# FFN up projections of the second block: seven products of sums of quarters in place of eight, in 14 of 16 chunks

## The chip, the cores and the metric

One core of one Trainium2 chip runs the kernel. The metric is device time in microseconds (us) of one execution; the median of the runs before the change is 3163.79 us (3163.3 to 3165.95, three runs).

## What is computed

Two transformer-like blocks of two layers each, on 512 tokens of 1024 features, in fp32. The second block, cut to what matters here:

```python
def squared_relu_mlp(x, w_up, w_down):
    return jnp.square(jax.nn.relu(x @ w_up)) @ w_down      # w_up 1024 x 4096, w_down 4096 x 1024

for i in range(2):
    y = dilated_attention_mixer(x, ...) if i == 0 else hgrn2_mixer(x, ...)
    x = layer_norm(DEEPNORM_ALPHA * x + y, ...)
    y = squared_relu_mlp(x, ffn_w_up[i], ffn_w_down[i])
    x = layer_norm(DEEPNORM_ALPHA * x + y, ...)
```

The first block has feed-forward layers of the same kind (`w_mlp1`, `w_mlp2`); the change leaves them alone.

## The kernel before

Every large product is made of three matmuls: each operand is split into a high and a low part (type fp32r), and `mm3` adds high x high, high x low and low x high into one PSUM bank (lines 165 to 167). The first operand of a matmul is the stationary one (its load is PEld in the profile), the second streams. A bank holds 128 x 512 fp32; the second block has eight banks (`pb2`).

Weights come in chunks of 1024 x 256 (or 512 x 512 for the down product): one DMA of 1 MB from SP's queue into `wr`, then `wchunk` makes the high part on ScalarE (line 193, `wh`) and the low part on VectorE (line 194, `wl`). `wr`, `wh` and `wl` have two buffers each. Small working tiles of 128 x 512 (`h`) have eight buffers, the large slots of 4 KB a partition (`t`) 27 in this block.

`ffn` (second block, called twice) calls `mlp` with width 512. There, hT are the normalised tokens, feature-major, as four pairs of tiles [128, 2, 512] for each of the two parts, made from four tiles of 128 tokens by `turn` (lines 434 and 436 scale, 253 and 254 split). `up` makes 128 features of the hidden layer: 8 x 3 matmuls into one bank, then relu and square on ScalarE (496, 497), and `split_to` on VectorE (249, 250). The first two chunks of 256 features run by halves of the tokens, so that the first half can start while the last tokens are still being normalised. Then come eight groups g: one up chunk, the down product of chunks 2g and 2g+1 (two halves c of the output, four token tiles each, 12 matmuls of 512 columns a bank, with two W2 loads), whose `sink` adds into the residual `xl` (1335, 1337), and one more up chunk. So the up chunk at the end of a group and the one at the start of the next stand back to back; there are 16 chunks, the last in the group before the last.

The order on each engine isn't written out by hand. The framework's scheduler lays the instructions out at build time, by readiness in its own model and by program order among what is ready, and each engine then works through its list in order. `later`, `tick` and `need` put off pieces of the program by counts.

Of the kernel before, what the change touches and what calls it, by code (L numbers as in the profile page):

```python
# [8 lines left out]
F32 = mybir.dt.float32  # L9
F32R = mybir.dt.float32r  # L10
I32 = mybir.dt.int32
AF = mybir.ActivationFunctionType
# [101 lines left out]
class Net:  # L114
# [367 lines left out]
        self.later(wait, go, key)  # L482


    def mlp(self, width, xT, w1, w2, ranges, tiles, sink, lag=3):
        nc = self.nc
        self.cut = 2

        def up(hc, w, f, c0, n):
            ps = self.bank()[:, :n]  # L490
            for k in range(8):
                self.mm3(ps, (w[0][:, k, f * 128:(f + 1) * 128], w[1][:, k, f * 128:(f + 1) * 128]),
                         self.kx(xT, k, c0, n), k == 0, k == 7)
            self.tick()
            r = self.half()[:, :n]
            nc.scalar.activation(r, ps, AF.Relu)  # L496
            nc.scalar.activation(r, r, AF.Square)  # L497
            self.split_to(hc[0][:, f, c0:c0 + n], hc[1][:, f, c0:c0 + n], r)

        hs = []  # L500

        def chunk():

            c0 = len(hs) * 256
            hs.append((self.slot([128, 2, width], F32R), self.slot([128, 2, width], F32R)))
            return hs[-1], self.wcols(w1, [(c0, c0 + 256)], alike=len(hs) > 2)

        def ups():
            if len(hs) < 16:
                h, w = chunk()  # L510
                for f in range(2):
                    for c0, n in ranges[1]:
                        up(h, w, f, c0, n)
                self.pump()

        first = [chunk(), chunk()]
        for c0, n in ranges[0]:
            self.need(*[("h", c) for c in range(c0, c0 + n, 128)])
            for h, w in first:
                for f in range(2):  # L520
                    up(h, w, f, c0, n)
        self.need()
        for g in range(8):
            ups()
            h = hs[2 * g:2 * g + 2]
            w = [None, None]
            for c, (tt, c0) in self.skew(tiles, lag if g == 7 else len(tiles)):
                if w[c] is None:
                    w[c] = self.wcols(w2[g * 512:(g + 1) * 512], [(c * 512, c * 512 + 512)], kt=4, alike=True)
                    self.pump()  # L530
                ps = self.bank()
                for k in range(4):
                    self.mm3(ps, (h[k // 2][0][:, k % 2, c0:c0 + 128], h[k // 2][1][:, k % 2, c0:c0 + 128]),
                             (w[c][0][:, k, :], w[c][1][:, k, :]), k == 0, k == 3)
                self.tick()
                sink(tt, c, g, ps)
            ups()
# [843 lines left out]
    def ffn(self, i, hT, last):  # L1381
        t = self.t
        rows = self.ln_rows("ffn", i)
        box = []

        def sink(j, c, g, ps):
            self.add_res(j, c * 512, 512, ps, g == 0)
            if g == 7:
                self.ln_stats(j, c)
                if c == 1:  # L1390
                    if not last and not box:
                        box.append(self.pairs(512))
                    self.ln_turn(j, "ffn", i, rows, None if last else box[0])

        self.mlp(512, hT, t["ffn_w_up_2"][i], t["ffn_w_down_2"][i], [[(0, 256), (256, 256)], [(0, 512)]],
                 [(j, j * 128) for j in range(4)], sink, 0 if last else 1)
        if last:
            self.need()
        return box[0] if box else None
# [531 lines left out]
```

## Time and profile before

| | us |
|---|---|
| median of three runs | 3163.79 |
| the profiled execution | 3167.63 |
| its span, first to last instruction | 3165.4 |
| TensorE / VectorE / ScalarE / GpSimd busy | 3102.1 / 1754.4 / 1344.6 / 376.5 |
| first FFN of the second block, chunk 2 to the end of group 6 | about 2215 to 2520 |
| second FFN, from chunk 2 on | about 2830 to 3130 |

A row of the trace gives a start, a duration, the engine, the line, what is written and read with the shapes, and in brackets how long the engine had been idle and what ended that. Matmul durations include the pipeline's depth and overlap; what a matmul costs in a stream is the distance between two starts.

### The profile page before, as it was taken

Reading aid. Unit: us, or ns where it says so; the run is one execution under the profiler, and the core shown is the slowest. Engines: PE = TensorE matmul, PEld = TensorE weight load, DVE = VectorE, ACT = ScalarE, POOL = GpSimd, SP = SyncE. Lnnn points to the kernel's source line nnn. Section 1 sums busy time; section 2 is a strip of 40 time slices with the busy share of each in tenths; the row PEclk is TensorE's granted clock in tenths of the full one; section 3 lists DMA queues with packets and bytes.
Section 4 is the critical chain, followed back from the end, with each engine's and each line's share of the span. In section 5 each row is a group of like instructions: output and inputs, shape, how many; then the busy total and the mean of one; then the engine's idle time right before and its main releaser. Section 6 shows DMA issues by size and latency. Waiting matters only on the chain.

```text
span 3165.4 us, 49101 instructions
## 1 busy us (share of the span) xinstructions
PE 3102.1 (98%) x20248; PEld 2633.0 (83%) x20248; DVE 1754.4 (55%) x3310; ACT 1344.6 (42%) x2533; POOL 376.5 (12%) x541
## 2 busy tenths in 40 slices
PE   7999999999999999999999999999999989989998
PEld 6977998888889879888888888888888878878887
DVE  5577454544456776555554544446444476664445
ACT  4566442222226665322245555555222266442222
POOL 4444000000004441000000000003000030030001
PEclk9999999999999999999999999999999999999999
DMA  7133223433322003233222222222333322222332
GB/s 224 44 104 107 68 84 118 131 109 108 119 73 67 12 14 94 93 97 103 93 97 94 80 68 67 81 70 67 106 96 104 98 67 67 89 81 98 93 94 79
DMA packets 246639, 281.67 MB, mean 89 GB/s; under 512 B 19534, under 2 KB 208400, under 8 KB 246416
## 3 DMA queue, kind: packets, MB, share of 16 engines
q1 hardware_dynamic: 244672, 273.54, 27.3%
q10 hardware_dynamic: 1584, 4.98, 0.4%
q8 instruction: 159, 2.61, 0.3%
q14 instruction: 64, 0.52, 0.1%
q0 software_dynamic: 160, 0.02, 0.0%
HBM read 276.42 MB, written 2.10 MB: 88 GB/s over the span
## 4 chain that ended last, share of the span: by engine, by line
PE 79%; issue 11%; DVE 5%; ACT 2%; POOL 1%; DMA 0%; SPq 0%; ACTq 0%; DVEq 0%; POOLq 0%
PE b L165 18%; PE b L167 17%; PE b L166 17%; PE s L165 5%; PE s L167 4%; PE s L166 4%; PE b L687 2%; PE b L671 2%; PE b L355 2%; PE s L649 1%; DVE t L254 1%; DVE wl L194 1%; PE b L1571 1%; PE b L1568 1%; PE b L1536 1%
## 5 line engine op out<-in xcount | busy, mean ns | idle before, releaser
L193 ACT ACTIVATE wh<-wr 128x2048 fp32r<-128x2048 f32 (+4 forms) x253 | 389.7, 1551 | 868.9 <-PE b L167 511.5
L194 DVE TENSOR_TENSOR wl<-wr,wh 128x2048 fp32r<-128x2048 f32 (+4 forms) x237 | 460.9, 1948 | 426.0 <-ACT wh L193 425.4
L165 PE MATMUL b<-wh,t 128*128 128x256 f32 (+2 forms) x2052 | 690.4, 337 | 0.8 <-ACT t L253 0.4
L166 PE MATMUL b<-wl,t 128*128 128x256 f32 (+2 forms) x2052 | 681.2, 332 | 4.1 <-DVE wl L194 4.1
L167 PE MATMUL b<-wh,t 128*128 128x256 f32 (+2 forms) x2052 | 681.3, 332 | 2.1 <-DVE t L254 2.1
L165 PE MATMUL b<-t,wh 128*128 128x512 f32 (+1 forms) x1696 | 625.9, 370 | 3.1 <-ACT t L253 3.0
L166 PE MATMUL b<-t,wh 128*128 128x512 f32 (+1 forms) x1696 | 616.8, 364 | 2.6 <-DVE t L254 2.6
L167 PE MATMUL b<-t,wl 128*128 128x512 f32 (+1 forms) x1696 | 617.5, 364 | 1.0 <-DVE wl L194 1.0
L165 PEld LDWEIGHTS b<-wh,t 128*128 128x128 f32 x2052 | 387.3, 189 | 45.6 <-issue 3.5
L166 PEld LDWEIGHTS b<-wl,t 128*128 128x128 f32 x2052 | 387.6, 189 | 42.3 <-DVE wl L194 4.9
L167 PEld LDWEIGHTS b<-wh,t 128*128 128x128 f32 x2052 | 387.1, 189 | 41.1 <-DVE t L254 3.0
L165 PEld LDWEIGHTS b<-t,wh 128*128 128x128 f32 x1696 | 321.7, 190 | 57.3 <-ACT t L253 4.0
L167 PEld LDWEIGHTS b<-t,wl 128*128 128x128 f32 x1696 | 322.2, 190 | 52.4 <-DVE wl L194 1.4
L166 PEld LDWEIGHTS b<-t,wh 128*128 128x128 f32 x1696 | 322.3, 190 | 50.4 <-DVE t L254 3.5
L249 DVE CAST t<-h 128x512 fp32r<-128x512 f32 (+1 forms) x176 | 66.2, 378 | 238.2 <-ACT h L497 238.0
L496 ACT ACTIVATE h<-b 128x512 f32<-128x512 f32 (+1 forms) x138 | 70.9, 513 | 219.1 <-PE b L167 219.1
L1202 DVE TENSOR_TENSOR h<-b,gate 128x512 f32<-128x512 f32 (+1 forms) x141 | 89.2, 632 | 113.7 <-PE b L167 113.7
L1337 DVE TENSOR_TENSOR xl<-xl,b 128x512 f32<-128x512 f32 x128 | 87.4, 684 | 112.3 <-PE b L167 112.3
L165 PE MATMUL s<-wh,t 128*128 128x256 f32 (+2 forms) x428 | 145.9, 341 | 2.0 <-ACT h L943 1.0
L166 PE MATMUL s<-wl,t 128*128 128x256 f32 (+2 forms) x428 | 143.0, 334 | 0.0
L167 PE MATMUL s<-wh,t 128*128 128x256 f32 (+2 forms) x428 | 142.9, 335 | 0.0
L1436 ACT ACTIVATE h<-b 32x512 f32<-32x512 f32 x192 | 113.3, 590 | 27.9 <-PE b L167 25.3
(365 smaller groups left out, 4504.7 us busy)
## 6 DMA issues: line engine op xcount, KB each, us to landing
wr<-in_w_mlp SPq DMA_DIRECT2D x64, 1024.0 KB, 5.3
wr<-in_w_mod SPq DMA_DIRECT2D x44, 1024.0 KB, 5.3
wr<-in_attn_w_in SPq DMA_DIRECT2D x36, 1024.0 KB, 5.1
wr<-in_ffn_w_up SPq DMA_DIRECT2D x32, 1024.0 KB, 5.4
wr<-in_ffn_w_down SPq DMA_DIRECT2D x32, 1024.0 KB, 4.9
wr<-in_hgrn_w_in SPq DMA_DIRECT2D x12, 1024.0 KB, 5.1
wr<-in_w_out SPq DMA_DIRECT2D x8, 640.0 KB, 5.5
wr<-in_w_in SPq DMA_DIRECT2D x4, 1024.0 KB
```

The costliest lines, as they stand in the source:

```text
L165: mm(out, a[0], b[0], start=start, stop=False)
L166: mm(out, a[0], b[1], start=False, stop=False)
L167: mm(out, a[1], b[0], start=False, stop=stop)
L193: nc.scalar.activation(hv, rv[:, k], AF.Copy)
L194: (self.aid if cut > 1 and m % 2 else nc.vector).tensor_sub(lv, rv[:, k], hv.bitcast(F32))
L249: self.nc.vector.tensor_copy(hi, src)
L355: self.nc.tensor.matmul(ps[32 * j:32 * j + 32], self.csil[:, k, :], raw[k], start=(k < 4 and not (more and j == 0)), stop=(k >= 4), tile_p ...
L496: nc.scalar.activation(r, ps, AF.Relu)
L671: nc.tensor.transpose(ps[:, kk, a * 128:(a + 1) * 128], u["P"][e, a][:, k0:k0 + 128], self.ident)
L1202: nc.vector.tensor_mul(tmp, ps, g[:, c0:c0 + n])
L1337: self.nc.vector.tensor_add(x, x, ps)
L1436: nc.scalar.activation(sw[32 * q:32 * q + 32], ps[32 * o:32 * o + 32], AF.Copy, scale=sc)
```

## The change

In the second block's FFNs, chunks 2 to 15 of the up product are computed as 2 x 2 x 2 blocks: halves of the 256 output features, halves of the 1024 input features and halves of the 512 tokens, with seven products of sums of quarters (Winograd's form of Strassen's method) in place of eight products of quarters. `token_sums` makes the four sums of token quarters once for each FFN, on VectorE, and splits them into parts; `weight_sums` loads a chunk, makes the four sums of weight quarters on VectorE (two in place), and splits the seven operands into two buffers of `wh` and `wl`; `seven` runs the products, each 4 x 3 matmuls of 256 columns, and adds them up out of PSUM on VectorE (one copy on ScalarE). Relu and square follow as before, and the split of the result has its high part now on ScalarE (`split_psum`).

```diff
--- before.py
+++ after.py
@@ -482,7 +482,96 @@
         self.later(wait, go, key)
 
 
-    def mlp(self, width, xT, w1, w2, ranges, tiles, sink, lag=3):
+
+
+    def token_sums(self, x, width):
+
+        nc = self.nc
+        n = width // 2
+        T = [[self.slot([128, 4, n], F32R) for _ in range(2)] for _ in range(4)]
+        view = lambda: self.half()[:, :2 * n].rearrange("p (k c) -> p k c", k=2)
+
+        def less(out, a, b):
+            d = view()
+            nc.vector.tensor_sub(out, a[0].bitcast(F32), b[0].bitcast(F32))
+            nc.vector.tensor_sub(d, a[1].bitcast(F32), b[1].bitcast(F32))
+            nc.vector.tensor_add(out, out, d)
+
+        def less_whole(out, a, t):
+            nc.vector.tensor_sub(out, a[0].bitcast(F32), t)
+            nc.vector.tensor_add(out, out, a[1].bitcast(F32))
+
+        for p in range(2):
+            quarter = lambda kh, th: [y[2 * kh + p][:, :, th * n:th * n + n] for y in x]
+            x11, x12, x21, x22 = (quarter(kh, th) for kh in range(2) for th in range(2))
+            t = [view() for _ in range(4)]
+            less(t[0], x12, x11)
+            less_whole(t[1], x22, t[0])
+            less(t[2], x22, x12)
+            less_whole(t[3], x21, t[1])
+            for i in range(4):
+                self.split_psum(*(y[:, 2 * p:2 * p + 2, :] for y in T[i]), t[i])
+        of = lambda i: lambda k: [y[:, k, :] for y in T[i]]
+        part = lambda kh, th: lambda k: [y[2 * kh + k // 2][:, k % 2, th * n:th * n + n] for y in x]
+
+        return [part(0, 0), part(1, 0), of(1), of(2), of(0), of(3), part(1, 1)]
+
+    def weight_sums(self, w, c0):
+
+        nc = self.nc
+        raw = self.raw().rearrange("p (k n) -> p k n", k=8)
+        nc.sync.dma_start(raw, w[:, c0:c0 + 256].rearrange("(k p) n -> p k n", p=128))
+        a11, a12, a21, a22 = (raw[:, 4 * kh:4 * kh + 4, 128 * f:128 * f + 128] for f in range(2) for kh in range(2))
+        s1, s2 = (self.half().rearrange("p (k n) -> p k n", k=4) for _ in range(2))
+        nc.vector.tensor_add(s1, a21, a22)
+        nc.vector.tensor_sub(s2, s1, a11)
+        nc.vector.tensor_sub(a21, a11, a21)
+
+        def parts(group):
+
+            at, out = 0 if self.apart else 8, []
+            hi, lo = (self.wp.tile([128, 2304], F32R, tag=tag, name=tag) for tag in ("wh", "wl"))
+            for src in group:
+                k, n = src.shape[1:]
+                hv, lv = (y[:, at:at + k * n].rearrange("p (k n) -> p k n", k=k) for y in (hi, lo))
+                nc.scalar.activation(hv, src, AF.Copy)
+                nc.vector.tensor_sub(lv, src, hv.bitcast(F32))
+                out.append((hv, lv))
+                at += k * n
+            return out
+
+        of = lambda y, k0=0, c0=0: lambda k: [part[:, k0 + k, c0:c0 + 128] for part in y]
+        first, p2, p3 = parts([raw[:, :, 0:128], s2, a21])
+        nc.vector.tensor_sub(a12, a12, s2)
+        p1, rest = parts([s1, raw[:, 4:8, :]])
+        return [of(first), of(first, 4), of(p2), of(p3), of(p1), of(rest, 0, 128), of(rest)]
+
+    def seven(self, A, B, n, out):
+
+        nc = self.nc
+        add = nc.vector.tensor_add
+        (m1, u2), (u3, u4) = ([x[:, :n], x[:, 512 - n:]] for x in (self.half(), self.half()))
+
+        def product(i):
+            ps = self.bank()[:, :n]
+            for k in range(4):
+                self.mm3(ps, A[i](k), B[i](k), k == 0, k == 3)
+            return ps
+
+        nc.scalar.activation(m1, product(0), AF.Copy)
+        add(out[0][0], product(1), m1)
+        add(u2, product(2), m1)
+        add(u3, product(3), u2)
+        self.tick()
+        ps = product(4)
+        add(u4, ps, u2)
+        add(out[1][1], ps, u3)
+        add(out[1][0], product(5), u3)
+        add(out[0][1], product(6), u4)
+        self.tick()
+
+
+    def mlp(self, width, xT, w1, w2, ranges, tiles, sink, lag=3, halves=False):
         nc = self.nc
         self.cut = 2
 
@@ -497,17 +586,33 @@
             nc.scalar.activation(r, r, AF.Square)
             self.split_to(hc[0][:, f, c0:c0 + n], hc[1][:, f, c0:c0 + n], r)
 
+        def up_halves(hc, c0):
+            n = width // 2
+            A = self.weight_sums(w1, c0)
+            rs = [self.half(), self.half()]
+            self.seven(A, sums, n, [[r[:, th * n:th * n + n] for th in range(2)] for r in rs])
+            for f, r in enumerate(rs):
+                nc.scalar.activation(r, r, AF.Relu)
+                nc.scalar.activation(r, r, AF.Square)
+                self.split_psum(hc[0][:, f, :], hc[1][:, f, :], r)
+
         hs = []
 
         def chunk():
 
             c0 = len(hs) * 256
             hs.append((self.slot([128, 2, width], F32R), self.slot([128, 2, width], F32R)))
+            if halves and len(hs) > 2:
+                return hs[-1], c0
             return hs[-1], self.wcols(w1, [(c0, c0 + 256)], alike=len(hs) > 2)
 
         def ups():
             if len(hs) < 16:
                 h, w = chunk()
+                if halves:
+                    up_halves(h, w)
+                    self.pump()
+                    return
                 for f in range(2):
                     for c0, n in ranges[1]:
                         up(h, w, f, c0, n)
@@ -520,6 +625,7 @@
                 for f in range(2):
                     up(h, w, f, c0, n)
         self.need()
+        sums = self.token_sums(xT, width) if halves else None
         for g in range(8):
             ups()
             h = hs[2 * g:2 * g + 2]
@@ -1393,7 +1499,7 @@
                     self.ln_turn(j, "ffn", i, rows, None if last else box[0])
 
         self.mlp(512, hT, t["ffn_w_up_2"][i], t["ffn_w_down_2"][i], [[(0, 256), (256, 256)], [(0, 512)]],
-                 [(j, j * 128) for j in range(4)], sink, 0 if last else 1)
+                 [(j, j * 128) for j in range(4)], sink, 0 if last else 1, halves=True)
         if last:
             self.need()
         return box[0] if box else None
```

## Rows read from the trace of the kernel before

**Rows 1.** The page, part 1: busy us, share of the span, instructions.

```profile
PE 3102.1 (98%) x20248; PEld 2633.0 (83%) x20248; DVE 1754.4 (55%) x3310; ACT 1344.6 (42%) x2533; POOL 376.5 (12%) x541
```

**Rows 2.** Windows, FFN loop: length, PE, PEld, DVE, ACT, POOL busy, clock, DMA, GB/s.

```profile
2300.00:2400.00 100.00, 100.00 (x443) 82.84 (x442) 41.66 (x45) 29.12 (x30) 0.00 (x0) 1.00 0.30 95
```

**Rows 3.** Groups by shape, 2226 to 2520: count | busy us, mean ns | idle before.

```profile
L165 PE MATMUL b<-t,wh 128*128 128x512 f32 x208 | 80.9, 389 | 0.0
...
L194 DVE TENSOR_TENSOR wl<-wr,wh 128x2048 fp32r<-128x2048 f32 x27 | 61.9, 2293 | 78.9 <-ACT wh L193 78.9
L193 ACT ACTIVATE wh<-wr 128x2048 fp32r<-128x2048 f32 x28 | 53.7, 1920 | 174.3 <-PE b L167 119.0 <-PE b L166 55.3
...
L165 PEld LDWEIGHTS b<-t,wh 128*128 128x128 f32 x208 | 39.1, 188 | 8.0
```

**Rows 4.** Timeline, PE, 512 columns: start, duration, instruction.

```profile
2840.95 0.39 PE L165 MATMUL b<-wh,t 128*128 128x512 f32 x1
...
2849.79 0.39 PE L165 MATMUL b<-wh,t 128*128 128x512 f32 x1
```

**Rows 5.** Timeline, PE, 256 columns, chunks 0 and 1.

```profile
2188.49 0.28 PE L165 MATMUL b<-t,wh 128*128 128x256 f32 x1
...
2196.30 0.28 PE L165 MATMUL b<-t,wh 128*128 128x256 f32 x1
```

**Rows 6.** Timeline, DVE, two operations back to back in the FFN loop.

```profile
2230.87 0.69 DVE L250 TENSOR_TENSOR t<-h,t 128x512 fp32r<-128x512 f32 x1
2231.47 0.68 DVE L1335 SCALAR_TENSOR_TENSOR xl<-xl,b 128x512 f32<-128x512 f32 x1
```

**Rows 7.** Timeline, ACT and DVE: 1024 elements, and 256 out of PSUM.

```profile
2132.37 1.05 ACT L1362 ACTIVATE t<-wr 128x1024 fp32r<-128x1024 f32 x1
2133.46 1.23 DVE L1363 TENSOR_TENSOR t<-wr,t 128x1024 fp32r<-128x1024 f32 x1 [0.20 <-ACT t L1362]
2140.35 0.42 DVE L1335 SCALAR_TENSOR_TENSOR xl<-xl,b 128x256 f32<-128x256 f32 x1 [0.43 <-PE b L167]
```

**Rows 8.** Timeline, ACT, second FFN: next chunk's weights, this chunk's relu.

```profile
2960.60 1.92 ACT L193 ACTIVATE wh<-wr 128x2048 fp32r<-128x2048 f32 x1 [3.95 <-PE b L166]
2962.42 0.57 ACT L496 ACTIVATE h<-b 128x512 f32<-128x512 f32 x1
```

**Rows 9.** Timeline, DVE: end of the norms in either FFN; two evictions together.

```profile
2202.76 0.41 DVE L250 TENSOR_TENSOR t<-h,t 128x256 fp32r<-128x256 f32 x1
...
2818.49 0.42 DVE L250 TENSOR_TENSOR t<-h,t 128x256 fp32r<-128x256 f32 x1
...
2828.87 0.49 DVE L249 CAST t<-h 128x256 fp32r<-128x256 f32 x2
2829.28 0.76 DVE L250 TENSOR_TENSOR t<-h,t 128x256 fp32r<-128x256 f32 x2
```

**Rows 10.** Timeline, PE: first matmul of chunk 2 in either FFN.

```profile
2214.88 0.40 PE L165 MATMUL b<-t,wh 128*128 128x512 f32 x1
...
2830.02 0.40 PE L165 MATMUL b<-t,wh 128*128 128x512 f32 x1
```

**Rows 11.** Windows around the last token tile's norm, first FFN.

```profile
2196.00:2201.00 5.00, 2.83 (x19) 2.10 (x18) 3.52 (x5) 3.04 (x9) 4.64 (x4) 0.92 0.00 0
2201.00:2206.00 5.00, 4.64 (x21) 4.64 (x22) 2.17 (x7) 0.47 (x2) 0.03 (x1) 0.50 0.00 0
```

**Rows 12.** Timeline, PE, behind it.

```profile
2201.36 0.58 PE L166 MATMUL b<-t,wh 128*128 128x256 f32 x1 [0.60 <-DVE t L254]
...
2206.44 0.41 PE L166 MATMUL b<-t,wh 128*128 128x256 f32 x1
2206.65 0.41 PE L167 MATMUL b<-t,wl 128*128 128x256 f32 x1
```

**Rows 13.** Timeline, PE, first matmul after transposes.

```profile
2188.06 0.36 PE L165 MATMUL b<-t,wh 128*128 128x256 f32 x1
2188.26 0.28 PE L166 MATMUL b<-t,wh 128*128 128x256 f32 x1
```

## The prediction

> **What bounds the kernel now.** I read the page first: TensorE is busy 98% of the span, VectorE 55%, ScalarE 42% [rows 1]. A busy TensorE need not be at its peak, so I next read the windows of the two FFN loops of the second block: in 100 us TensorE never stops, at the full granted clock (2.4 GHz), while VectorE is busy 41.66 us, ScalarE 29.12 us and GpSimd not at all [rows 2]. So in this stretch time is the number of matmuls by their spacing, and VectorE and ScalarE are free to the extent that nothing waits for them. The groups of one stretch give the pieces: 48 matmuls of 512 columns a chunk, one weight load each, one split of a whole weight chunk 1.92 us on ScalarE and then 2.29 us on VectorE [rows 3]. Spacing is read from starts in the timeline, not from durations, which overlap. 39 matmuls of 512 columns pass between the two rows of [rows 4]: 8.84 / 39 = 0.2267 us each. 66 of 256 columns pass between those of [rows 5]: 7.81 / 66 = 0.1183 us.
>
> **What the change removes.** An up chunk of 256 features is 2 x 8 x 3 = 48 matmuls of 512 columns, 48 x 0.2267 = 10.88 us. After it, seven products of 4 x 3 = 12 matmuls of 256 columns, 84 x 0.1183 = 9.94 us. It isn't the eighth that the product count promises (1.36 us), since a column costs more in short matmuls: 0.462 ns against 0.443. 28 chunks (14 in each of two FFNs) give 28 x 0.94 = **26.4 us off**, if TensorE goes on without waits.
>
> A rule of the Trainium skill (TensorE: Matmul & The Clock Gate, Back-to-back issue gap) gives N/2.4 + 2.5 ns, 109 and 216 ns here, and by it an estimated 1.19 us a chunk, 33 us in all. The trace's 0.1183 and 0.2267 are above both, and I use those.
>
> **What it adds on VectorE and ScalarE, in each chunk.** VectorE issues 512-element operations 0.60 us apart [rows 6], takes 1.23 us for 1024 elements and 0.42 us for 256 out of PSUM [rows 7], some 0.09 us of each under the next. A chunk now has nine of 512 (three sums of the weights, one update in place, three splits, two splits of the result), two splits of 1024 and seven additions of 256: 9 x 0.60 + 2 x 1.14 + 7 x 0.33 = 10.0 us. With two W2 splits (2 x 2.2) and eight residual additions (8 x 0.60), a group of two chunks and 96 down matmuls has 29.2 us of VectorE in 2 x 9.94 + 96 x 0.2267 = 41.6 us, 70% (now 42%). In the back-to-back pair of chunks it is tighter: 20.0, less 4.1 done ahead under the down matmuls and 1.2 left to those that follow, plus 2.2 for W2, is 16.9 in 19.9 us. ScalarE has two copies of 1.05 us [rows 7], nine operations of 512 elements of about 0.57 us [rows 8] and one of half that, 7.5 us in a chunk of 9.94. Both are covered by TensorE, so I cost the work itself at nothing; without the cover a chunk costs up to 10.0 - 9.94 = 0.1 us more, and what remains is where it stands in line. W1 loads keep their size, place and number on SP's queue. Buffers: six of the eight h tiles a chunk; in the 27 slots 8 for hT, 8 for the sums, 2 for the norm's rows and up to 8 for h, 26: no wait from there.
>
> **Where TensorE can wait: the two weight buffers.** wh and wl have two buffers each. A chunk now takes both (products 0 to 3 from one, 4 to 6 from the other), so in place of four uses a group has six. Behind every run of sevens comes W2's first half: its ScalarE copy may start only when product 3 is done, and products 4 to 6 last 36 x 0.1183 = 4.26 us. The chain is about 0.17 (end of the last matmul after the next one's start) + 1.92 + 2.29 = 4.38 us [rows 3], and only the second matmul needs its end: nearly nothing if both engines are free. What is queued around it are the additions out of PSUM (VectorE) and the eviction of the chunk before (ScalarE). Bounds: 0 and about 1.5 us, a ScalarE backlog of two 0.57 us operations and an addition. I take one addition ahead of it, 0.33 us, since by the count ScalarE's eviction and second split (six of 0.57, 0.57 and 1.05, 5.0 us) fit before product 3 ends (48 x 0.1183 = 5.68). There are 8 such places in each FFN (after chunk 2, six pairs, after chunk 15): 16 x 0.33 = **5.3 us on**. From one chunk to the next the same count leaves room: 1.05 [rows 7] + 1.23 in 4.26 us.
>
> **The token sums.** This is the largest term against. Their 20 additions and 8 splits on VectorE are 28 x 0.60 = 16.8 us, and all need the second half of the tokens: VectorE has done the last splits of hT, and an eviction behind them, at 2202.76 + 0.41 = 2203.17 in the first FFN, 2818.91 in the second [rows 9]. TensorE comes to chunk 2 at 2214.88 and 2830.02 [rows 10], only 11 us later. In that time VectorE also has four evictions of chunks 0 and 1, two of which take 0.49 + 0.76 less the overlap, 1.17 us [rows 9], so 2.3. Upper bound: the first weight split (1.23) stands behind all sums: 16.8 + 2.3 + 1.23 = 20.3 us, TensorE waits until 2223.5 and 2839.2, that is 8.6 + 9.2 = 17.8 us. Lower bound: the weight split slips in ahead, and products 0 and 1, which need no sums, run on time; product 2 needs the second half of its sum 3.55 us after the start, and 26 of the 28 operations, 2.3, 1.23 and 0.69 for its weights are done at 2223.0 and 2838.7: 4.6 + 5.1 = 9.7 us. I take **9.7 us on**: [rows 8] show that issue order isn't program order, as a weight copy of the next chunk stands ahead of a relu of the present one, and a ready split can go where a sum waits for the one before it.
>
> Such a wait has a second price. Before the second half of the tokens TensorE is busy only 2.83 of 5 us, and the granted clock is then 0.50 (1.2 GHz) [rows 11]; matmuls stand 0.21 us apart until 2206.65 [rows 12]. That is some 25 x 0.095 = 2.4 us. The new wait is about as long: 2 x 2.4 = **4.8 us on** (0 if the clock holds).
>
> **Sum:** -26.4 + 5.3 + 9.7 + 4.8 = -6.6 us. The profiled execution took 3167.6 us (span 3165.4), 3.8 above the median of the runs; so 3161.0 for it, and 3157.2 as the median of runs.
>
> **The rivals.**
> - *The sums stand ahead of the weights* (program order on VectorE): 17.8 in place of 9.7, +1.5 us, 3165.3. For it: the sums come first in the code and seldom wait; against it, [rows 8]. Chance 0.18.
> - *Slower: the two weight buffers become the bound.* If W2's copy stands behind the evictions on ScalarE, or its split behind those on VectorE, each of the 16 places costs 1.5 us, 24 in place of 5.3: +12.1 us, 3175.9. It decides from 0.74 us a place (5.3 + 6.6 over 16). For it: now the first W2 copy begins as soon as a buffer falls free, and the chain has no slack left; against it, ScalarE is a third free. Chance 0.20.
> - *Nothing waits but for the sums, and the clock holds:* -26.4 + 9.7 + 1.6 (0.1 a place) = -15.1, 3148.7. Chance 0.13.
> - *The change doesn't bring fewer microseconds of matmul:* 7 product changes a chunk may cost what a change of operand does after transposes, 0.20 against 0.12 [rows 13]: 0.08 x 7 x 28 = 16 us, 3173. In 24-matmul groups [rows 5] no such gap is seen. Chance 0.05.
> - *Weight loads come out:* a load takes 0.188 us [rows 3], longer than the 0.1183 between matmuls [rows 5], so today it is hidden whole. If not, 36 more loads a chunk cost 36 x 0.188 - 0.94 = 5.8 us, 163 us in all, 3320. Chance 0.01. The Trainium skill (TensorE: Matmul & The Clock Gate, Part 3, The mechanism) says that a load overlaps running matmuls only when its row group differs; all here use all rows, so by that rule this rival would hold. The trace disagrees, with the two numbers of the rival's first sentence.
>
> **How the numbers follow.** The forecast has 0.43. About 0.2% (6.3 us) is what a measurement can tell from no change, so the limits are 3157.5 and 3170.1. The forecast lies on the first, and I give 0.23 of it to faster, 0.20 to same. Faster: 0.23 + 0.13 = 0.36. Same: 0.20 + 0.14 of the first rival + 0.02 of the second = 0.36. Slower: 0.04 + 0.18 + 0.05 + 0.01 = 0.28. Range: from 3146, below the best case by a little, to 3176, the second rival. The likeliest case alone is 3151 to 3164.
>
> **What would show it.** Right: 256-column matmuls of the sevens 0.118 us apart, 84 a chunk; one TensorE wait of 4 to 9 us in each FFN before or in chunk 2, with the clock at half behind it; waits of a few tenths before W2's first half, ended by VectorE's wl split. Wrong: a wait in chunk after chunk, above all over 0.7 us at W2; spacing above 0.13 within a product; VectorE busy over 90% in the loops; or no wait at chunk 2 at all, which would mean that TensorE was given down matmuls meanwhile.

## The result, and the profile after

The changed kernel takes 3199.94 us (median of 4 runs, 3199.01 to 3200.78) against 3163.55 for the kernel before (3162.39 to 3165.95): a ratio of 1.0114, 95% interval 1.0101 to 1.0126. It is 36.4 us slower, where 6.6 us faster was forecast, and outside the forecast's range. The profiled execution took 3199.01 us, with a span of 3196.8.

The page after, part 1, and the group of part 5 with the sevens' first matmuls (before: [rows 1]):

```profile
PE 3082.0 (96%) x21256; PEld 2660.1 (83%) x21256; DVE 1960.3 (61%) x3730; ACT 1432.7 (45%) x2745; POOL 374.7 (12%) x541
...
L165 PE MATMUL b<-t,wh 128*128 128x256 f32 (+1 forms) x2032 | 675.7, 334 | 50.1 <-ACT wh L537 46.9
```

TensorE is busy 20 us less than before, and the span is 31 us longer: the matmuls became cheaper as forecast, and TensorE now stands still. The waits of TensorE after (us in all, times, longest) say for what. The first row is new, the second was there before with 9.0 us:

```profile
PE b L165 <- ACT wh L537: 46.9, 14, 16.5
PE b L428 <- DVE t L1425: 9.7, 5, 4.7
```

L537 copies the high half of a chunk's weights and weight sums. Fourteen waits are two long ones, one in each FFN (16.45 and 16.51 us), and twelve short ones, one in each back-to-back pair of chunks (13.9 us together). **The long one**, first FFN, timelines of VectorE, ScalarE and TensorE:

```profile
2200.09 0.41 DVE L254 TENSOR_TENSOR t<-h,t 128x256 fp32r<-128x256 f32 x1
2200.43 0.41 DVE L250 TENSOR_TENSOR t<-h,t 128x256 fp32r<-128x256 f32 x1
2204.44 0.29 DVE L249 CAST t<-h 128x256 fp32r<-128x256 f32 x1 [3.60 <-ACT h L586]
...
2207.27 1.23 DVE L538 TENSOR_TENSOR wl<-wr,wh 128x1024 fp32r<-128x1024 f32 x1 [2.08 <-ACT wh L537]
...
2210.20 0.43 DVE L250 TENSOR_TENSOR t<-h,t 128x256 fp32r<-128x256 f32 x1
2210.55 0.69 DVE L496 TENSOR_TENSOR h<-t 128x512 f32<-128x512 f32 x1
...
2226.39 2.48 DVE L254 TENSOR_TENSOR t<-h,t 128x512 fp32r<-128x512 f32 x4
2228.80 0.68 DVE L526 TENSOR_TENSOR h<-wr 128x512 f32<-128x512 f32 x1
2229.51 0.69 DVE L527 TENSOR_TENSOR h<-h,wr 128x512 f32<-128x512 f32 x1
...
2230.31 0.62 ACT L537 ACTIVATE wh<-h 128x512 fp32r<-128x512 f32 x1
...
2230.99 0.58 PE L165 MATMUL b<-t,wh 128*128 128x256 f32 x1 [16.45 <-ACT wh L537]
```

hT is complete at 2200.50 (first row), and VectorE is through with the eviction behind it at 2200.84, yet the first token sum (L496) starts at 2210.55, right behind the split of the third of four later evictions of chunks 0 and 1, and VectorE is idle for 3.60 and 2.08 us in between. The weight split of products 0 and 1 (L538) does slip in ahead, at 2207.27. The sums and their splits run to 2228.8, and only then come chunk 2's weight sums s1 and s2 (L526, L527), which need no token at all. Product 2 waits for the copy of s2. The sums are done at 2228.87, so the last 2.1 us of the 16.45 are the price of s1 and s2 standing behind them. The windows around it show the second price, and the clock that comes back (columns as in [rows 2]):

```profile
2211.00:2216.00 5.00, 3.53 (x30) 3.33 (x29) 4.23 (x9) 1.77 (x4) 0.00 (x0) 1.00 0.00 0
2216.00:2231.00 15.00, 0.01 (x1) 0.02 (x1) 14.96 (x26) 5.51 (x11) 0.00 (x0) 0.52 0.00 0
2231.00:2237.00 6.00, 6.00 (x27) 5.92 (x28) 4.29 (x8) 1.98 (x3) 0.00 (x0) 0.50 0.26 55
2237.00:2241.00 4.00, 4.00 (x36) 4.00 (x36) 2.82 (x4) 1.44 (x1) 0.00 (x0) 1.00 0.46 180
```

**The short one**, in a pair of chunks, the same three timelines:

```profile
2358.00 0.42 DVE L568 TENSOR_TENSOR h<-b,h 128x256 f32<-128x256 f32 x1
2358.34 0.68 DVE L526 TENSOR_TENSOR h<-wr 128x512 f32<-128x512 f32 x1
2359.27 0.68 DVE L527 TENSOR_TENSOR h<-h,wr 128x512 f32<-128x512 f32 x1
...
2360.97 1.14 ACT L596 ACTIVATE h<-h 128x512 f32<-128x512 f32 x2
2362.01 1.13 ACT L253 ACTIVATE t<-h 128x512 fp32r<-128x512 f32 x2
2363.05 0.61 ACT L537 ACTIVATE wh<-h 128x512 fp32r<-128x512 f32 x1
...
2362.28 0.28 PE L167 MATMUL b<-t,wl 128*128 128x256 f32 x1
2363.72 0.39 PE L165 MATMUL b<-t,wh 128*128 128x256 f32 x1 [1.16 <-ACT wh L537]
```

The second chunk's s1 and s2 stand behind outputs of the first (L568), and the copy of s2, which VectorE ended at 2359.95, stands on ScalarE behind the first chunk's squares and copies until 2363.05. A group of two chunks and 96 down matmuls, between its W1 issues on SP's queue, then lasts 43.41 us:

```profile
2284.74 4.60 SPq L523 DMA_DIRECT2D wr<-in_ffn_w_up  x2
2328.15 4.60 SPq L523 DMA_DIRECT2D wr<-in_ffn_w_up  x2
```

That is as long as before (43.52 us between W1 issues at 2262.69 and 2306.21; 2 x 10.88 + 96 x 0.2267 = 43.5), where 41.6 was forecast.

### The profile page after: what moved, and what is told of

The parts are those of the page before. It is cut to its first block, busy times and chain, and to the rows that moved or that the text cites. A ratio compares the mean times of both kernels' runs of the same rounds, so it can differ in the third digit from the quotient of the medians.

```text
span 3196.8 us, 51853 instructions
## 1 busy us (share of the span) xinstructions
PE 3082.0 (96%) x21256; PEld 2660.1 (83%) x21256; DVE 1960.3 (61%) x3730; ACT 1432.7 (45%) x2745; POOL 374.7 (12%) x541
## 4 chain that ended last, share of the span: by engine, by line
PE 83%; DVE 7%; ACT 4%; issue 3%; POOL 1%; DMA 1%; SPq 0%; ACTq 0%; DVEq 0%; POOLq 0%
PE b L165 19%; PE b L167 19%; PE b L166 19%; PE s L165 4%; PE s L167 4%; PE s L166 4%; PE b L793 2%; PE b L777 2%; DVE t L254 1%; PE b L355 1%; PE s L755 1%; DVE wl L194 1%; ACT wh L537 1%; PE b L1677 1%; PE b L1674 1%
## 5 line engine op out<-in xcount | busy, mean ns | idle before, releaser
L165 PE MATMUL b<-t,wh 128*128 128x256 f32 (+1 forms) x2032 | 675.7, 334 | 50.1 <-ACT wh L537 46.9
L166 PE MATMUL b<-t,wh 128*128 128x256 f32 (+1 forms) x2032 | 664.0, 327 | 3.3 <-DVE t L254 3.3
L167 PE MATMUL b<-t,wl 128*128 128x256 f32 (+1 forms) x2032 | 662.5, 328 | 1.0 <-DVE wl L194 1.0
L193 ACT ACTIVATE wh<-wr 128x2048 fp32r<-128x2048 f32 (+4 forms) x225 | 335.8, 1505 | 592.7 <-PE b L167 275.2
L194 DVE TENSOR_TENSOR wl<-wr,wh 128x2048 fp32r<-128x2048 f32 (+4 forms) x209 | 397.5, 1906 | 272.0 <-ACT wh L193 271.5
L165 PEld LDWEIGHTS b<-t,wh 128*128 128x128 f32 x2032 | 386.7, 191 | 92.9 <-ACT wh L537 52.4
L166 PEld LDWEIGHTS b<-t,wh 128*128 128x128 f32 x2032 | 387.9, 191 | 33.8 <-DVE t L254 3.9
L167 PEld LDWEIGHTS b<-t,wl 128*128 128x128 f32 x2032 | 386.1, 191 | 34.6 <-DVE wl L194 1.4
L249 DVE CAST t<-h 128x256 fp32r<-128x256 f32 (+1 forms) x120 | 42.6, 356 | 181.5 <-ACT h L586 181.2
L537 ACT ACTIVATE wh<-wr 128x1024 fp32r<-128x1024 f32 (+1 forms) x84 | 75.3, 911 | 126.1 <-PE b L167 77.4
```

What stands on the lines that cost most here:

```text
L165: mm(out, a[0], b[0], start=start, stop=False)
L166: mm(out, a[0], b[1], start=False, stop=False)
L167: mm(out, a[1], b[0], start=False, stop=stop)
L193: nc.scalar.activation(hv, rv[:, k], AF.Copy)
L194: (self.aid if cut > 1 and m % 2 else nc.vector).tensor_sub(lv, rv[:, k], hv.bitcast(F32))
L249: self.nc.vector.tensor_copy(hi, src)
```

## The experiments

Theory 1: the loss is order. The sums, and s1 and s2, stand too late on VectorE though their data are there. The rivals: VectorE or ScalarE has too much work wherever it stands, or a seven costs something that isn't seen as a wait. The kernels are numbered in the order in which they were run, and stand here by question.

### The two orders, one at a time

The first kernel emits the token sums earlier:

```
+            if halves and c0:                       # ahead of chunks 0, 1, second 256 tokens
+                sums = self.token_sums(xT, width)
...
-        sums = self.token_sums(xT, width) if halves else None
```

> Edit: the token sums are emitted as soon as hT's last columns stand, ahead of chunk 0's and 1's products over the second 256 tokens, not behind them. Theory 1 (order): the 16.45 us that TensorE waits at product 2 of each FFN is sums that began 10 us after their data stood, because their buffers come after those of the last evictions in program order, with chunk 2's weight sums behind them in turn. Then the sums begin at hT's end, s1 of chunk 2 comes some 8 us earlier and the wait falls to 6 to 10 us in each FFN: 3183 to 3189 us. Theory 2 (VectorE's load): VectorE has that much work before it anyhow, the place of the sums only exchanges them with the evictions, and product 2 starts within 3 us of where it did: 3194 to 3201 us. The pairs' waits of 1.16 us in the second chunk stay in both.

Measured: 3186.79 us, ratio 1.0076 (1.0061 to 1.0091). Theory 1, for the part it was about. VectorE's first sum and TensorE's wait:

```profile
2201.61 0.68 DVE L496 TENSOR_TENSOR h<-t 128x512 f32<-128x512 f32 x1
...
2222.73 0.58 PE L167 MATMUL b<-t,wl 128*128 128x256 f32 x1 [11.23 <-DVE wl L538]
```

The sums start with hT's end, at 2201.61. The 11.23 us that are left (9.7 in the second FFN) lie at product 0, whose weight split now stands behind the whole block of sums and ends at 2222.68; in the kernel after, two products were done by then, but the third had to wait until 2230.99.

The second emits a pair's second weight sums earlier:

```
-            A = self.weight_sums(w1, c0)
+            A = ahead.pop(c0) if c0 in ahead else self.weight_sums(w1, c0)
+            if c0 // 256 % 2 and c0 < 3840:
+                ahead[c0 + 256] = self.weight_sums(w1, c0 + 256)
```

> Edit: of two chunks that follow one another without W2 between them, the second's weight sums, copies and splits are emitted ahead of the first's products. The token sums stay where they are. Theory 1 (order of the buffers): the 1.16 us wait at product 3 of each second chunk, and the slower spacing behind it, come from s1 standing behind the first chunk's outputs though its raw weights were loaded 20 us before. It goes, about 1.7 us in each of 12 pairs: 3177 to 3184 us. Theory 2 (ScalarE): the two engines have no time for the copies in that stretch, so the wait moves to another tile and stays at about 1 us: 3195 to 3203 us. Theory 3: the copies ahead delay the first chunk's evictions, so that its outputs or W2's first half come late: over 3203 us. The wait of 16.45 us at the start stays in all.

Measured: 3177.92 us, ratio 1.0050 (1.0035 to 1.0065): 22 us less than the change. (The wait is at product 2, counted from 0; the text above says 3.) All twelve short waits are gone, only the two long ones stay (waits of TensorE):

```profile
PE b L165 <- ACT wh L537: 33.0, 2, 16.5
```

And a group, by the W1 issues on SP's queue, now takes 41.70 us:

```profile
2286.74 4.38 SPq L523 DMA_DIRECT2D wr<-in_ffn_w_up  x2
2328.44 4.37 SPq L523 DMA_DIRECT2D wr<-in_ffn_w_up  x2
```

43.41 - 41.70 is 1.71 us a pair, 12 x 1.71 = 20.5. ScalarE does the same work in either order, so its load isn't the cause.

### What holds s1 back: the buffer or the place

The twelfth kernel gives s1 and s2 a buffer of another pool:

```
-        s1, s2 = (self.half().rearrange("p (k n) -> p k n", k=4) for _ in range(2))
+        both = self.slot([128, 2, 512])
+        s1, s2 = (both[:, j, :].rearrange("p (k n) -> p k n", k=4) for j in range(2))
```

> Edit: s1 and s2 of every chunk in one 4 KB slot of the pool that holds hT and h, and not in two buffers of the pool of eight that the first chunk's outputs also use; the program's order stays that of the change. It tells what holds s1 back in the second chunk of a pair. Theory 1a (the eight buffers, given out in program order): the 1.16 us waits vanish as in the second run, 3177 to 3184 us. Theory 1b (the order in which the program emits the work, whatever the buffer: a ready operation of the later chunk isn't put ahead of the earlier chunk's outputs on VectorE): the waits stay or grow and the time is 3197 to 3206 us. The start's wait of 16.45 us stays in both.

Measured: 3253.35 us, ratio 1.0281 (1.0264 to 1.0298), slower than either theory had it. s1 now comes even later, behind all of the first chunk's outputs and its evictions, and a pair waits 3.18 us. VectorE and TensorE:

```profile
2372.34 0.42 DVE L563 TENSOR_TENSOR h<-b,h 128x256 f32<-128x256 f32 x1 [1.18 <-PE b L167]
2372.68 0.68 DVE L254 TENSOR_TENSOR t<-h,t 128x512 fp32r<-128x512 f32 x1
2373.28 0.68 DVE L527 TENSOR_TENSOR t<-wr 128x512 f32<-128x512 f32 x1
...
2375.41 0.58 PE L165 MATMUL b<-t,wh 128*128 128x256 f32 x1 [3.18 <-ACT wh L538]
```

The windows before, at and behind the wait:

```profile
2366.00:2371.00 5.00, 5.00 (x44) 5.00 (x43) 3.20 (x6) 2.63 (x6) 0.00 (x0) 1.00 0.18 68
2371.00:2375.40 4.40, 1.23 (x11) 1.02 (x9) 3.19 (x7) 2.70 (x6) 0.00 (x0) 0.89 0.01 2
2375.40:2381.00 5.60, 5.59 (x25) 5.49 (x26) 3.86 (x6) 1.58 (x2) 0.00 (x0) 0.50 0.19 30
```

The waits grew, as Theory 1b has it. In either kernel s1 is late by its place among VectorE's instructions: here VectorE is idle for 1.18 us up to 2372.34, with s1's weights loaded. What sets that place isn't shown, though: by the prediction's count 26 of the other pool's 27 slots are taken as it is, so s1 may have waited for a buffer there too. The price grows faster than the wait. Against the change it is 53.4 us, 4.45 a pair: 2.02 us of longer wait, and 25 matmuls at half clock, 0.21 apart for 0.118 [rows 12], 25 x 0.095 = 2.4 us. Why the build orders the work later with this buffer than with the other stays open.

### What the sums cost by themselves

The third kernel leaves the token sums out, so that it computes other values:

```
-        return [part(0, 0), part(1, 0), of(1), of(2), of(0), of(3), part(1, 1)]
+        return [part(0, 0), part(1, 0), part(1, 1), part(0, 1), part(1, 0), part(0, 1), part(1, 1)]   # and no sums
```

> Leaves out the token sums: plain quarters of hT stand in for them, so the products have the same shapes and weights and other values. Theory 1: the start then waits for chunk 2's weight sums alone, which come behind the last evictions: a wait of 0 to 4 us in place of 16.45, no half clock behind it: 3162 to 3172 us. If the start's wait were the weights' own (a late load, the copies), it would stay above 10 us and the time at 3185 to 3200. The pairs' waits stay, and a group's period stays at 43.4 us.

Measured: 3160.25 us, ratio 0.9987 (0.9977 to 0.9996). The long waits are gone, the twelve short ones stay (14.0 us). It lies 2 us below the interval forecast; -26.4 for the sevens and +20.5 for the pairs would be -5.9, and -3.4 came.

The eleventh has the sums and no sevens (the same condition stands in `ups`):

```
-            if halves and len(hs) > 2:
+            if halves and len(hs) > 99:             # no chunk by sevens; the sums stay
```

> All 32 chunks in the ordinary way; the token sums are computed where the change has them and nobody reads them. It shows the price of the block of sums on VectorE alone. Theory 1: chunk 2's products need only hT and wait for W1's splits and for the evictions behind the block; the fourth run lost some 8.3 us per FFN in such waits: 3172 to 3186 us. Theory 2 (the sums cost only because product 2 reads them and VectorE's gaps take them otherwise): 3163 to 3168 us.

Measured: 3190.35 us, ratio 1.0083 (1.0068 to 1.0098), 24 us for sums that nobody reads and 4 us above Theory 1's range. So the price isn't only that product 2 needs them: a block of 17 us on VectorE delays whatever is queued behind it, here W2's splits (waits of TensorE):

```profile
PE b L166 <- DVE wl L194: 16.8, 3, 6.5
```

In the kernel before, that row has 4.1 us; new are two waits for a split of W2, 6.46 and 6.47 us, one in each FFN.

### Both orders together, and the sums spread

The ninth kernel has the edits of the first and the second.

> Edit: the first and the second run's edits together, all sums on VectorE, 14 of 16 chunks by sevens. If the two costs are separate places, as Theory 1 has it, the gains add: 3199.9 less 13.1 (first run) less 22 (second run) is 3164.8, so 3162 to 3168 us, about the time of the kernel before: what is left is the 10 us of sums per FFN that nothing covers while product 2 waits. If one edit undoes the other, or they cure the same time: 3172 us or more.

Measured: 3167.53 us, ratio 1.0004 (0.9994 to 1.0013). The gains add; the two places are separate. What is left is 11.2 and 9.7 us of wait at the start, so the change in its own 14 of 16 chunks comes out even once its orders are mended.

The fourth kernel has the same edits, and chunk 2 in the ordinary way as well (`len(hs) > 3` for `len(hs) > 2`).

> Edit: token sums ahead of the second 256 tokens as in the first run, weights ahead as in the second, and chunk 2 made in the ordinary way, so that 13 of 16 chunks go by sevens. Theory 1: chunk 2's ordinary products (10.9 us) cover what is left of the sums, so that neither the start nor the pairs wait: 26 chunks by 0.94 us less than 3163.6, 24 us, less up to 6 us of small waits: 3139 to 3146 us. Theory 2 (VectorE's load at the start): the evictions that now stand behind the sums delay W2's first group by about 5 us in each FFN: 3147 to 3156 us. If sevens cost something in every chunk that the trace doesn't show as a wait: 3157 to 3170 us.

Measured: 3166.84 us, ratio 1.0011 (1.0002 to 1.0020): 21 us above Theory 1's range. It lies in the range named for a cost in every chunk, but a group takes 41.70 us here too (W1 issues at 2360.28 and 2401.98), so that theory falls. The loops run without a wait, but the block of sums now stands ahead of chunk 0's and 1's evictions and of W2's splits. TensorE's waits there:

```profile
2219.89 1.19 PE L165 MATMUL b<-wh,t 128*128 128x512 f32 x2 [4.39 <-DVE t L249]
2223.95 0.80 PE L167 MATMUL b<-t,wl 128*128 128x512 f32 x1 [2.87 <-DVE wl L194]
```

Moving a block only chooses who waits behind it. The next kernels, the fifth and the sixth, cut the sums into 8 pieces (two or three sums and a split each), one piece behind one product:

```
+            pieces += [lambda i=i, piece=piece: piece(i) for i in range(4)]
...
                 sink(tt, c, g, ps)
+                if halves and g == 0:
+                    for _ in range(1):
+                        if pieces:
+                            pieces.pop(0)()
```

> Edit: weights ahead as in the second run; chunks 2 and 3 in the ordinary way, so that 12 of 16 chunks go by sevens; the token sums cut into 8 pieces of 2 or 3 sums and a split each, one behind each tile of W2's first group. The fourth run (13 of 16) still waited some 4.4, 2.9 and 1.0 us per FFN because 17 us of sums stood in one block ahead of evictions and splits. Theory 1 (only the places of the sums and of s1 cost, a seven itself keeps its 0.94 us a chunk): with the sums in VectorE's gaps nothing waits, and the time is that of before less 24 chunks by 0.94, 22.6 us: 3139 to 3144 us. Theory 2 (VectorE's total load in the first group, sums included, is too much wherever they stand): 3148 to 3158 us. Theory 3 (sevens have a cost of their own that the trace doesn't show as a wait): 3158 us or more.

> Edit: as the fifth run, with chunk 3 by sevens too, so that the 8 pieces must end by its product 2, some 33 us after chunk 2's start. Theory 1: VectorE's idle share of that stretch (about 0.3 of 45 us, 13 us) falls short of 17 us of sums by some 4 us: a wait of 2 to 5 us in each FFN against 1.9 us gained by the two chunks: 3141 to 3150 us. Theory 2 (load): 3150 to 3160 us.

Measured: 3150.11 us with 12 chunks of 16 (ratio 0.9948, 0.9933 to 0.9963) and 3156.12 with 13 (0.9970, 0.9958 to 0.9981). Faster than before at last, but both in the range of Theory 2, too much work for VectorE: 22.6 us were there to gain with 12 and 15.6 came. All pieces with 12 chunks, and six of the eight with 13, stood under W2's first group, and the copy and split of its second half came late (1.13 and 1.02 us of wait with 12 chunks, 3.63 with 13, in each FFN).

The seventh and the tenth put the pieces elsewhere. The cut is from the seventh, where GpSimd makes half of the sums; the tenth has VectorE for both:

```
+                    for _ in range(1 if halves and c0 else 0):   # from hT's end on, behind each up product
+                        pieces.pop(0)()
...
+            eng, sp = (nc.gpsimd, nc.gpsimd) if p else (nc.vector, nc.vector)
```

> Edit: as the sixth run, with the sums and splits of one half of the features on GpSimd, which is idle in the FFN (its 128x512 adds take 1.36 us in the profile, so 14 of them 19 us beside VectorE's 14 by 0.60). Pieces one behind each ordinary product from hT's end on. Theory 1: VectorE's part falls to 8.4 us and fits, nothing waits: 3137 to 3142 us. Theory 2 (the two engines slow one another, or the sums are late all the same): 3146 to 3158 us.

> Edit: the seventh run with all of the sums on VectorE again, in the same places (pieces one behind each ordinary product from hT's end on, halves of the features in turn): it tells GpSimd's part from that of the places. Theory A (GpSimd is what the seventh run gained by): 14 operations of 0.60, 8.4 us, come back to VectorE in each FFN and wait as in the sixth run: 3150 to 3157 us. Theory B (the places): VectorE was slowed beside GpSimd anyhow (an add of 0.68 us took 1.78 there), so that moving half gave little: 3141 to 3146 us.

Measured: **3142.83 us** with half of the sums on GpSimd, ratio 0.9925 (0.9909 to 0.9942), the fastest kernel here: 22.9 of 24.5 us, 0.8 us above Theory 1's range. With all sums on VectorE in the same places it is 3147.42, ratio 0.9942 (0.9925 to 0.9958), between Theory A and Theory B and nearer to B. The tenth has as many sums on VectorE as the sixth and is some 9 us faster, so most of what looked like too much work there was its place; GpSimd gave some 4 us more, though the two intervals overlap. In the seventh kernel TensorE stands still for half a microsecond in 45 us of sums, and nothing in a group behind it:

```profile
2200.00:2245.00 45.00, 44.45 (x233) 38.77 (x234) 41.80 (x46) 18.12 (x27) 20.53 (x14) 0.96 0.22 71
...
2307.84:2349.57 41.73, 41.73 (x266) 37.82 (x264) 30.54 (x47) 18.00 (x27) 0.00 (x0) 1.00 0.31 101
```

The eighth has GpSimd's half too, but all 14 chunks, with two pieces behind each of the last four products of chunks 0 and 1.

> Edit: 14 of 16 chunks by sevens as in the change, weights ahead, one half of the sums and splits on GpSimd, two pieces behind each of the last four products of chunks 0 and 1. Theory 1: T1's two halves stand after 7 operations of each engine (4.2 us on VectorE, 9.5 us on GpSimd), about when product 2 is due, the later ones 2 to 4 us late: a wait of 2 to 5 us in each FFN, 3164 less 26.4 and up to 14 for waits and the clock behind them: 3142 to 3151 us. Theory 2 (the two engines slow one another): a wait of 8 us or more as in the first run, 3157 to 3168 us.

Measured: 3175.98 us, ratio 1.0031 (1.0020 to 1.0042), slower than both theories. TensorE waits twice in chunk 2:

```profile
2215.33 0.39 PE L167 MATMUL b<-t,wl 128*128 128x256 f32 x1 [2.41 <-DVE wl L546]
2229.90 0.58 PE L165 MATMUL b<-t,wh 128*128 128x256 f32 x1 [11.70 <-ACT wh L545]
```

VectorE was busy from 2204 on, partly because its additions were held up by GpSimd's (last section), and s1 of chunk 2 again came behind nearly all of the sums, at 2226.23. With 14 chunks no arrangement tried here got the sums done between hT's end and product 2.

## Why the prediction was wrong

- **The matmuls: right.** 28 x 0.94 = 26.4 us off. With nothing in the way a group takes 41.70 us (second run) where 41.6 was computed, so neither short matmuls nor product changes nor weight loads cost more than said: (41.70 - 96 x 0.2267) / 168 = 0.1187 us a matmul, weight loads of 0.19 us hidden. The rivals on product changes and on weight loads fall. With the second falls the rule named there from the list in the Trainium skill (TensorE: Matmul & The Clock Gate, Part 3, The mechanism), as it stands; the text above that list also lets a load into a background weight buffer go ahead of running matmuls, and no run here tells whether that is what hides it.
- **The two weight buffers at W2: too dear.** 5.3 us were put on. The group of 41.70 leaves 0.06 us over 41.64, so some 0.4 us a FFN at most, and no wait there in the trace after. The slower rival, which hung on this place, falls too.
- **The token sums: the step that failed.** "VectorE has done the last splits of hT" was taken as the time at which the sums start. They started 9.7 us later, at their place behind three evictions of chunks 0 and 1, whose data TensorE had yet to make; the prediction had counted the work of these evictions (2.3 us) and not their time. Why the build put the sums there, by buffers or by order alone, stays open. The argument that issue order isn't program order [rows 8] held for one weight split (2207.27), but not for the sums, s1 and s2; s1 and s2, which the sum for product 2 left out, stood behind all sums. 33.0 us came for 9.7, beyond the upper bound of 17.8. That bound was too low even with the sums at hT's end: the first run waited 20.9 us.
- **The clock behind the wait: right.** 27 matmuls in 6 us at 0.50 in the first FFN, 27 x 0.095 = 2.6 us; twice that is 5.2 for 4.8.
- **From one chunk to the next: the other step that failed.** The words "the same count leaves room" set the first copy and split of the next chunk (2.28 us) into 4.26 us and did not ask where s1, s2 and their copies stand: not in the time after product 3, but behind the first chunk's outputs and, on ScalarE, behind its squares. A share of 70% of VectorE said nothing on that. 20.5 us came for 0, and no rival had them; only among the signs of being wrong did a wait in chunk after chunk stand.

Together -26.4 + 33.0 + 5.2 + 20.5 = 32.3 us, of 36.4 measured. The sum is read from traces, and the two profiled executions lie only 31.4 us apart (3199.01 - 3167.63), as the one before took 4.1 us more than its median; so the 4 us that are missing from 36.4 need no place of their own, though none is excluded. Mended in the order of the weights, with the sums spread and half of them on GpSimd, the change brings 22.9 of the 24.5 us of its arithmetic, in 13 of 16 chunks.

## What to carry to other kernels

New work on an engine that is half idle starts at its place in that engine's order, not when its data stand; so for each new operation name the instruction ahead of it and the time of that one, above all for sums that need nothing recent. A block of work moved as a whole only changes who waits behind it: cut it into pieces of two or three operations and put each behind a product that lasts longer. And a wait of 3 us costs more than 3 us, since the clock has to come back: a pair with 3.18 us of wait in the twelfth kernel costs 4.45 us more than one with 1.16.

## What the runs showed of the hardware

VectorE's operations on SBUF are held up by GpSimd's. From the seventh kernel, GpSimd and VectorE:

```profile
2219.78 1.38 POOL L519 TENSOR_TENSOR t<-h,t 128x512 fp32r<-128x512 f32 x1 [3.60 <-ACT t L518]
2233.68 1.48 POOL L502 TENSOR_TENSOR h<-t,h 128x512 f32<-128x512 f32 x1
...
2219.91 1.78 DVE L519 TENSOR_TENSOR t<-h,t 128x512 fp32r<-128x512 f32 x1
2221.62 1.37 DVE L249 CAST t<-h 128x256 fp32r<-128x256 f32 x1
2233.93 0.67 DVE L1463 SCALAR_TENSOR_TENSOR xl<-xl,b 128x512 f32<-128x512 f32 x1
```

The same split takes 0.68 us alone and 1.78 when it starts 0.13 us behind GpSimd's, and then ends 0.53 us after it: as if it waited for GpSimd's end and ran then. The residual addition, which reads one operand from PSUM, takes its usual 0.67 us beside one. The Trainium skill (SBUF — State Buffer, Who interferes with whom) says that a VectorE instruction with two SBUF inputs contends with a GpSimd instruction that reads SBUF, and that the one that issues second blocks; the trace agrees, with these 1.78 and 0.67 us. A cast, with one input, is held up in this kernel as well: the one at 2221.62, beside a GpSimd subtraction that runs from 2221.11 to 2222.85, takes 1.37 us for the 0.29 of the kernel after.

The clock fell behind waits of different lengths to the same level: 0.50 (1.2 GHz) for some 6 us after 16.45 us of idle TensorE, and for some 5.6 us after 3.18. Over a stretch with a 1.16 us wait in it, in the kernel after, the row keeps 1.00:

```profile
2328.00:2371.00 43.00, 41.82 (x263) 37.56 (x262) 30.32 (x47) 18.00 (x26) 0.00 (x0) 1.00 0.30 99
```
